# Attention's products with the values as float32r passes over a whole head

## The chip, the cores and the metric

The kernel runs on one core of a Trainium2 chip. The time is the device time of one execution in microseconds. The profile covers one execution; its span runs from the first to the last recorded instruction of the core.

## What is computed

Two layers, each `h += ½·SwiGLU(norm(h))`, `h += mixer(norm(h))`, `h += ½·SwiGLU(norm(h))`, then a last norm, for one sequence of 512 positions and width 1024, in float32. The change lies in layer 0's mixer, an attention with 8 heads of width 128 in which a small indexer picks 128 keys for each query:

```python
q, k, v, qi, ki, wi = jnp.split(h @ w_in, A_SPLITS, axis=-1)
...
_, idx = lax.top_k(score, top_k)
...
logits = (jnp.einsum('bthe,btkhe->bhtk', qb, kg) * scale + bias)
logits = jnp.where(valid[:, None], logits, -jnp.inf)
p = jax.nn.softmax(logits, axis=-1)
o = jnp.einsum('bhtk,btkhe->bthe', p, vg)
...
return out @ w_out
```

The kernel gathers nothing: it computes all causal logits and adds a mask of the chosen keys.

## The kernel before

Activations are held transposed: eight tiles H of 128 features by 512 positions. Most products are written as three TensorE passes in float32r: `mul3` (L345) multiplies the high part of the weights with the high and the low part of the activations, and the low part of the weights with the high part of the activations. A pair of parts comes from `split` (L369): ScalarE copies the number into a float32r tile (the high part), VectorE subtracts that from the number (the low part). Weights stream in 512 KB pieces on SyncE's queue; for each piece ScalarE writes the high part (L184) and another engine the low part (L187): VectorE as a rule, and GpSimd from L779 until the end of the heads (L945). A piece serves eight calls of `take`, and pieces are converted ahead of use, in the order of the program.

The schedule is written by hand: every engine runs its instructions in the order in which the program issues them, and waits on semaphores where data is not there yet.

In `mixer_a` (L694) the program first computes the indexer's scores and, for each block of 128 queries but the first, 16 rounds of `max8` and `match_replace` on VectorE, which leave the mask. These steps wait in a list, `W.background`, out of which each weight conversion takes some. Between them `v_half` (L817) computes the values for 512 of the 1024 columns at a time, and ScalarE copies them out of PSUM with the norm's scale (L829) into V, four float32 tiles of 128 positions by 1024.

Then come the heads. The list `blocks` (L920) has 32 entries, a head and a block b of 128 queries; block b sees (b+1)·128 keys. One round of the loop (L922) issues, in this order:

- `normalize` (L885) for the entry two rounds back: VectorE's reciprocal (L888) and a scaling of the probabilities (L889);
- `logits` (L869) for this round's entry: TensorE's product of queries and keys in float32 (L872), VectorE's scale and bias (L876), VectorE's mask and maximum (L879), VectorE's negation of the maximum (L881), ScalarE's exponential with its sum (L882);
- two steps of `filler` (L857): three-pass products for the queries and keys of later heads, later for the output projection `out_first`;
- `turn` (L891) for the entry three rounds back: b+1 transposes on TensorE (L896) into one bank, and ScalarE's copy into the tile pT (L898);
- one more filler step in odd rounds;
- `values` (L903) for the entry four rounds back: b+1 float32 products of the values with pT (L908) into 128 columns of the bank po. After a head's last block `split` writes its output from po into two float32r tiles, oh and ol (L911 to L913).

```python
mm(po[0][:, b * P:(b + 1) * P], V[j][:, h * P:(h + 1) * P], pT[:, j * P:(j + 1) * P],
   start=j == 0, stop=j == b)
```

PSUM has eight banks in two rings of four: "aux" serves logits and transposes, "acc" the fillers and po. The output projection reads oh and ol of all heads; after the loop its remaining products follow (L943 to L955).

Of the kernel before, what the change touches and what calls it, by code (L numbers as in the profile page):

```python
# [12 lines left out]
F32 = mybir.dt.float32  # L13
F32R = mybir.dt.float32r
I32 = mybir.dt.int32
AF = mybir.ActivationFunctionType
ALU = mybir.AluOpType
PSUM = bass.MemoryType.PSUM

P = 128  # L20
D = 1024
S = 512
KD = D // P
NT = S // P
# [217 lines left out]
def tile_trunk(ctx: ExitStack, tc, specs_out, xT, wst, gT, gl, rel, onehot, bu, bv, lng, lnb, wspT, bsp, out):  # L242
    nc = tc.nc
# [9 lines left out]
    def uname(s):  # L253
        counter[0] += 1
        return f"{s}_{counter[0]}"

    def pad(pool, size):

        pool.tile([P, size // 4], F32, name=uname("pad"))
# [3 lines left out]
    mm = nc.tensor.matmul  # L263
    def bank(tag="acc"):
        return psum.tile([P, 512], F32, tag=tag, bufs=4, name=uname(tag))
# [103 lines left out]
    def split(src, hi, lo):  # L369
        nc.scalar.activation(hi, src, AF.Copy)  # L370
        nc.vector.tensor_tensor(lo, src, hi.bitcast(F32), op=ALU.subtract)
# [322 lines left out]
    def mixer_a(dist, next_norm):  # L694
# [8 lines left out]

        with ExitStack() as stack:
            ap = stack.enter_context(tc.tile_pool(name="mixa", bufs=1))
            V = [ap.tile([P, D], F32, name=f"v{t}") for t in range(NT)]
            score = {b: ap.tile([P, (b + 1) * P], F32, name=f"score{b}") for b in range(1, NT)}
            pad(ap, 288)
            rq = ap.tile([P, NT], F32, name="rq")
            caus = ap.tile([P, P], F32, name="caus")  # L710
            nc.gpsimd.memset(caus, 0.0)
# [3 lines left out]
            R = {}  # L715
# [43 lines left out]
            with tc.tile_pool(name="mixai", bufs=1) as ip:  # L759
                ki = ip.tile([P, S], F32, name="ki")  # L760
                kh = ip.tile([P, S], F32R, name="kh")
                kl = ip.tile([P, S], F32R, name="kl")
                wiT = ip.tile([IDX_DIM + IDX_HEADS, S], F32, name="wiT")
                wi = ip.tile([P, NT, IDX_HEADS], F32, name="wi")
                lo, hi = slice(0, IDX_DIM), slice(IDX_DIM, P)
                wr = slice(IDX_DIM, IDX_DIM + IDX_HEADS)
                nc.vector.tensor_copy(wiT[wr], kw[wr])
                nc.vector.tensor_tensor(ki[lo], kw[lo], rb[lo], op=ALU.mult)
                nc.scalar.activation(ki[hi], ki[lo], AF.Copy)
                split(ki, kh, kl)  # L770
                pad(ip, 128)
                qs = []
                for h in range(IDX_HEADS):
                    a, b = (lo, hi) if h % 2 == 0 else (hi, lo)
                    t = ip.tile([P, S], F32R, name=f"qs{h}")
                    nc.scalar.activation(t[a], pq[h // 2][a], AF.Copy)
                    nc.vector.tensor_tensor(t[b], pq[h // 2][a], t[a].bitcast(F32), op=ALU.subtract)
                    qs.append(t)
                W.lo_engine = nc.gpsimd  # L779

                for i, _ in enumerate(projections(range(1), "acc")):
                    if i != KD:
                        continue
                    rc = R["c"]
                    nc.vector.tensor_scalar(rq, rc, P ** -0.5, None, op0=ALU.mult)
                    pw = bank("aux")
                    for t in range(NT):
                        nc.tensor.transpose(pw[:, t * IDX_HEADS:(t + 1) * IDX_HEADS], wiT[wr, t * P:(t + 1) * P],
                                            ident[wr, wr])
                    for t in range(NT):  # L790
                        nc.vector.tensor_scalar(wi[:, t], pw[:, t * IDX_HEADS:(t + 1) * IDX_HEADS], rc[:, t:t + 1],
                                                rc[:, t:t + 1], op0=ALU.mult, op1=ALU.mult)
                    w = wi.rearrange("p t h -> p (t h)")
                    nc.vector.tensor_scalar(w, w, IDX_HEADS ** -0.5, None, op0=ALU.mult)

                def score_one(b, h):
                    n = (b + 1) * P
                    sc = score[b]
                    ps = bank()
                    q = qs[h][:, b * P:(b + 1) * P]  # L800
                    mm(ps[:, :n], q, kh[:, :n], start=True, stop=False)
                    mm(ps[:, :n], q, kl[:, :n], start=False, stop=True)
                    rl = ip.tile([P, S], F32, tag="rl", bufs=3, name=uname("rl"))
                    nc.scalar.activation(rl[:, :n], ps[:, :n], AF.Relu, scale=IDX_DIM ** -0.5)
                    w = wi[:, b, h:h + 1]
                    if h == 0:
                        nc.vector.tensor_scalar(sc, rl[:, :n], w, None, op0=ALU.mult)
                    else:
                        nc.vector.scalar_tensor_tensor(sc, rl[:, :n], w, sc, op0=ALU.mult, op1=ALU.add)
                    if h == IDX_HEADS - 1:  # L810
                        nc.gpsimd.affine_select(out=sc[:, b * P:], in_=sc[:, b * P:], compare_op=ALU.is_ge,
                                                fill=NOT_CAUSAL, base=0, pattern=[[-1, P]], channel_multiplier=1)
                        W.background = interleave(W.background, top_k(b))

                todo = [(b, h) for b in range(1, NT) for h in range(IDX_HEADS)]

                def v_half(c, tag):  # L817
                    banks = [bank(tag) for _ in range(NT)]
                    for k in range(KD):
                        wh, wl = W.take(*[spec_a(k, 2 * D + c * 512 + i * P) for i in range(4)])  # L820
                        for t in range(NT):
                            xh, xl = XH[k][:, t * P:(t + 1) * P], XL[k][:, t * P:(t + 1) * P]
                            mm(banks[t], xh, wh, start=k == 0, stop=False)
                            mm(banks[t], xl, wh, start=False, stop=False)
                            mm(banks[t], xh, wl, start=False, stop=k == KD - 1)
                        for _ in range(min(3, len(todo))):
                            score_one(*todo.pop(0))
                    for t in range(NT):
                        nc.scalar.activation(V[t][:, c * 512:(c + 1) * 512], banks[t], AF.Copy,  # L829
                                             scale=R["c"][:, t:t + 1])  # L830

                W.pops = 2
                v_half(0, "aux")
                W.pops = 6
                v_half(1, "acc")
                assert not todo

            vp = stack.enter_context(tc.tile_pool(name="mixav", bufs=1))
            pad(vp, 352)
            O = {}  # L840
# [50 lines left out]
            def turn(h, b):  # L891
                n = (b + 1) * P
                pr, _ = prob.pop((h, b))
                ps = bank("aux")
                for j in range(b + 1):
                    nc.tensor.transpose(ps[:, j * P:(j + 1) * P], pr[:, j * P:(j + 1) * P], ident)  # L896
                pT = vp.tile([P, S], F32, tag="pT", bufs=2, name=uname("pT"))
                nc.scalar.activation(pT[:, :n], ps[:, :n], AF.Copy)  # L898
                turned[h, b] = pT

            po = [None]

            def values(h, b):  # L903
                if b == 0:
                    po[0] = first[3] if first else bank()
                pT = turned.pop((h, b))
                for j in range(b + 1):
                    mm(po[0][:, b * P:(b + 1) * P], V[j][:, h * P:(h + 1) * P], pT[:, j * P:(j + 1) * P],  # L908
                       start=j == 0, stop=j == b)
                if b == NT - 1:  # L910
                    oh = vp.tile([P, S], F32R, name=f"oh{h}")  # L911
                    ol = vp.tile([P, S], F32R, name=f"ol{h}")
                    split(po[0], oh, ol)  # L913
                    O[h] = (oh, ol)

            for h in range(3):
                load_bias(h)
# [4 lines left out]
            for i in range(len(blocks) + lag + 1):  # L922
                if 2 <= i < len(blocks) + 2:
                    normalize(*blocks[i - 2])
                if i < len(blocks):
                    logits(*blocks[i])
                    h, b = blocks[i]
                    if b == NT - 1 and h + 3 < HEADS:
                        load_bias(h + 3)
                filler(2)  # L930
                if lag <= i < len(blocks) + lag:
                    turn(*blocks[i - lag])
                filler(i % 2)
                if i > lag:
                    values(*blocks[i - lag - 1])
                if i == 4:
                    W.pops = 1

# [309 lines left out]
```

## Time and profile before

| | |
|---|---|
| median of 3 runs | 2093.56 us (2093.43 to 2094.03) |
| profiled execution | 2093.53 us, span 2091.7 us |
| TensorE matmul | 2076.6 us busy, 99% of the span |
| TensorE weight load | 1844.4 us, 88% |
| VectorE | 1476.7 us, 71% |
| ScalarE | 894.3 us, 43% |
| GpSimd | 78.1 us, 4% |
| DMA | 209.72 MB, 100 GB/s on average |

In the trace TensorE's instructions are PE (matmul) and PEld (weight load), VectorE is DVE, ScalarE is ACT, GpSimd is POOL. A float32 product stands as two PE instructions. A matmul's recorded length includes its way through the array, and matmuls overlap; what one costs in a row of others is the distance from start to start. VectorE and ScalarE instructions also overlap a little, so there, too, the distance between starts counts. The stretch with the heads runs from 488 to 592 us of the span.

### The profile page before, as it was taken

What the parts mean: (1) busy time and instruction counts of PE and PEld (TensorE: products, weight loads), DVE (VectorE), ACT (ScalarE), POOL (GpSimd) and SP (SyncE); (2) the same over time, 40 slices, a digit from 0 to 9 for tenths busy, and PEclk for the clock granted to TensorE, in tenths of its full rate; (3) what the DMA queues carried; (4) which work ended last, traced back from release to release, by engine and by line L of the source; (5) the groups of instructions that cost most, each with busy time, mean ns of one, the idle gap of its engine ahead of it and who ended that gap; (6) DMA issues with size and microseconds to landing.
All of it is one profiled execution on the core that took longest, in us unless ns stands there. A gap on an engine that the chain in (4) does not pass through costs nothing.

```text
span 2091.7 us, 29771 instructions
## 1 busy us (share of the span) xinstructions
PE 2076.6 (99%) x12252; PEld 1844.4 (88%) x12252; DVE 1476.7 (71%) x2046; ACT 894.3 (43%) x1157; POOL 78.1 (4%) x57
## 2 busy tenths in 40 slices
PE   8999999999999999999999999999999999999998
PEld 7989898888888999898989999888888888989897
DVE  7768686597767678677968677645846466778676
ACT  6535344434446345354625344432323245535253
POOL 0000000143200000000000000000000000000000
PEclk9999999999999999999999999999999999999999
DMA  4233332222123222222333222422222222323321
GB/s 174 98 117 109 112 110 92 100 96 90 68 72 110 101 101 101 101 101 82 111 106 107 101 102 81 152 91 91 91 101 83 89 91 91 111 94 109 110 93 71
DMA packets 59001, 209.72 MB, mean 100 GB/s; under 512 B 6824, under 2 KB 6872, under 8 KB 58736
## 3 DMA queue, kind: packets, MB, share of 16 engines
q1 hardware_dynamic: 55584, 198.73, 27.4%
q0 software_dynamic: 1408, 5.38, 0.8%
q10 hardware_dynamic: 1872, 3.70, 0.5%
q8 instruction: 96, 1.57, 0.3%
q14 instruction: 41, 0.34, 0.1%
HBM read 205.67 MB, written 4.74 MB: 101 GB/s over the span
## 4 chain that ended last, share of the span: by engine, by line
PE 97%; DVE 2%; ACT 1%; issue 0%; ACTq 0%; DVEq 0%
PE acc L348 16%; PE acc L349 16%; PE acc L350 16%; PE aux L348 12%; PE aux L350 12%; PE aux L349 12%; PE acc L990 1%; PE aux L992 1%; PE aux L990 1%; PE acc L992 1%; PE acc L991 1%; PE aux L991 1%; PE aux L1040 1%; PE acc L908 1%; PE aux L872 1%; PE aux L896 0%
## 5 line engine op out<-in xcount | busy, mean ns | idle before, releaser
L187 DVE TENSOR_TENSOR wlo<-raw,whi 128x1024 fp32r<-128x1024 f32 (+1 forms) x382 | 463.4, 1218 | 296.7 <-ACT whi L184 296.3
L184 ACT ACTIVATE whi<-raw 128x1024 fp32r<-128x1024 f32 (+1 forms) x409 | 426.2, 1050 | 470.4 <-PE acc L349 192.0
L348 PE MATMUL acc<-xh,whi 128*128 128x512 f32 (+1 forms) x864 | 299.2, 346 | 1.7 <-ACT xh L309 1.6
L349 PE MATMUL acc<-xl,whi 128*128 128x512 f32 (+1 forms) x864 | 289.5, 335 | 1.1 <-DVE xl L310 1.1
L350 PE MATMUL acc<-xh,wlo 128*128 128x512 f32 (+1 forms) x864 | 289.1, 335 | 0.0
L348 PE MATMUL aux<-xh,whi 128*128 128x256 f32 (+1 forms) x616 | 196.9, 320 | 0.0
L350 PE MATMUL aux<-xh,wlo 128*128 128x256 f32 (+1 forms) x616 | 196.5, 319 | 0.0
L349 PE MATMUL aux<-xl,whi 128*128 128x256 f32 (+1 forms) x616 | 196.4, 319 | 0.0
L348 PEld LDWEIGHTS acc<-xh,whi 128*128 128x128 f32 x864 | 164.8, 191 | 20.0 <-ACT xh L309 2.6
L349 PEld LDWEIGHTS acc<-xl,whi 128*128 128x128 f32 x864 | 165.0, 191 | 18.7 <-DVE xl L310 2.0
L350 PEld LDWEIGHTS acc<-xh,wlo 128*128 128x128 f32 x864 | 164.8, 191 | 16.9
L348 PE MATMUL acc<-th,whi 128*128 128x256 f32 x608 | 172.4, 284 | 0.0
L350 PE MATMUL acc<-th,wlo 128*128 128x256 f32 x608 | 172.1, 283 | 0.0
L349 PE MATMUL acc<-tl,whi 128*128 128x256 f32 x608 | 172.0, 283 | 0.0
L348 PE MATMUL aux<-th,whi 128*128 128x256 f32 x544 | 154.0, 283 | 0.0
L349 PE MATMUL aux<-tl,whi 128*128 128x256 f32 x544 | 154.0, 283 | 0.0
L350 PE MATMUL aux<-th,wlo 128*128 128x256 f32 x544 | 154.0, 283 | 0.0
L348 PE MATMUL acc<-yh,whi 128*128 128x512 f32 x328 | 127.7, 389 | 0.0
L349 PE MATMUL acc<-yl,whi 128*128 128x512 f32 x328 | 127.7, 389 | 0.0
L348 PE MATMUL aux<-yh,whi 128*128 128x512 f32 x328 | 127.6, 389 | 0.0
L349 PE MATMUL aux<-yl,whi 128*128 128x512 f32 x328 | 127.6, 389 | 0.0
L350 PE MATMUL acc<-yh,wlo 128*128 128x512 f32 x328 | 127.6, 389 | 0.0
(292 smaller groups left out, 4404.9 us busy)
## 6 DMA issues: line engine op xcount, KB each, us to landing
raw<-in_wst SPq DMA_DIRECT2D x372, 512.0 KB, 3.2
dist<-dist_rows ACTq DMA_DIRECT2D x8, 320.0 KB, 4.2
h<-in_xT SPq DMA_DIRECT2D x8, 256.0 KB, 6.4
tb<-dist POOLq DMA_DIRECT2D x8, 256.0 KB, 3.9
bias<-in_bv POOLq DMA_DIRECT2D x1, 1536.0 KB, 7.5
raw<-in_wst SPq DMA_DIRECT2D x2, 256.0 KB, 3.5
wT<-in_wspT POOLq DMA_DIRECT2D x1, 512.0 KB, 9.3
bs<-in_bsp POOLq DMA_DIRECT2D x1, 512.0 KB, 11.4
```

The source lines that it names most:

```text
L184: self.nc.scalar.activation(hi[:, s], src[:, s], AF.Copy)
L187: self.lo_engine.tensor_tensor(lo[:, s], src[:, s], hi[:, s].bitcast(F32), op=ALU.subtract)
L348: mm(ps, wh, xh, start=first, stop=False, **kw)
L349: mm(ps, wh, xl, start=False, stop=False, **kw)
L350: mm(ps, wl, xh, start=False, stop=last, **kw)
L872: mm(ps[:, :n], QK[h, 0][:, b * P:(b + 1) * P], QK[h, 1][:, :n], start=True, stop=True)
L908: mm(po[0][:, b * P:(b + 1) * P], V[j][:, h * P:(h + 1) * P], pT[:, j * P:(j + 1) * P], start=j == 0, stop=j == b)
L990: mm(banks[t], xh, wh, start=k == 0, stop=False)
L991: mm(banks[t], xl, wh, start=False, stop=False)
L992: mm(banks[t], xh, wl, start=False, stop=k == KD - 1)
L1040: mm(ps[:, t * P:(t + 1) * P], V[t][:, d * P:(d + 1) * P], wT[:, g, :], start=True, stop=True)
```

## The change

The values are kept in two float32r parts instead of one float32 tile: for each half of the columns a high and a low tile, with four heads, four blocks of positions and 128 columns each. ScalarE writes the high part from PSUM with the norm's scale, VectorE the low part from PSUM, the scale and the high part. The transposed probabilities of a head are also kept in two parts, in tiles with 13 places of 128 columns. Block b's transposes go to places b, b+3, ..., b+3b, so that the queries which see key block j lie next to each other from place 4j on. ScalarE copies the transposes into the high tile as before (now rounded), and VectorE writes the low tile from PSUM and the high tile. The products are done once a head, after its last block: for each key block j three passes over all queries from block j on, 512, 384, 256 and 128 columns wide, which accumulate in one bank. The head's output parts go where the head's values were.

```diff
-            V = [ap.tile([P, D], F32, name=f"v{t}") for t in range(NT)]
             score = {b: ap.tile([P, (b + 1) * P], F32, name=f"score{b}") for b in range(1, NT)}
-            pad(ap, 288)
+            pad(ap, 448)
+            V = [[ap.tile([P, 4, NT, P], F32R, name=f"v{part}{c}") for part in "hl"] for c in range(2)]
+            pad(ap, 352)
...
                     for t in range(NT):
-                        nc.scalar.activation(V[t][:, c * 512:(c + 1) * 512], banks[t], AF.Copy,
-                                             scale=R["c"][:, t:t + 1])
+                        ps, r = banks[t].rearrange("p (h d) -> p h d", d=P), R["c"][:, t:t + 1]
+                        hi, lo = (v[:, :, t] for v in V[c])
+                        nc.scalar.activation(hi, ps, AF.Copy, scale=r)
+                        nc.vector.scalar_tensor_tensor(lo, ps, r, hi.bitcast(F32), op0=ALU.mult, op1=ALU.subtract)
...
-                pT = vp.tile([P, S], F32, tag="pT", bufs=2, name=uname("pT"))
-                nc.scalar.activation(pT[:, :n], ps[:, :n], AF.Copy)
-                turned[h, b] = pT
-
-            po = [None]
-
-            def values(h, b):
                 if b == 0:
-                    po[0] = first[3] if first else bank()
-                pT = turned.pop((h, b))
-                for j in range(b + 1):
-                    mm(po[0][:, b * P:(b + 1) * P], V[j][:, h * P:(h + 1) * P], pT[:, j * P:(j + 1) * P],
-                       start=j == 0, stop=j == b)
-                if b == NT - 1:
-                    oh = vp.tile([P, S], F32R, name=f"oh{h}")
-                    ol = vp.tile([P, S], F32R, name=f"ol{h}")
-                    split(po[0], oh, ol)
-                    O[h] = (oh, ol)
+                    turned[h] = [vp.tile([P, 13, P], F32R, tag="pT" + part, bufs=2, name=uname("pT")) for part in "hl"]
+
+                hi, lo = (x[:, b:4 * b + 1:3] for x in turned[h])
+                ps = ps[:, :n].rearrange("p (j q) -> p j q", q=P)
+                nc.scalar.activation(hi, ps, AF.Copy)
+                nc.vector.tensor_tensor(lo, ps, hi.bitcast(F32), op=ALU.subtract)
+
+            def values(h):
+                po = first[3] if first else bank()
+                ph, pl = (x.rearrange("p a q -> p (a q)") for x in turned.pop(h))
+                vh, vl = (x[:, h % 4] for x in V[h // 4])
+                for j in range(NT):
+                    s, m = slice(j * P, S), slice(4 * j * P, (3 * j + NT) * P)
+                    o, end = po[:, s], j == NT - 1
+                    mm(o, vh[:, j], ph[:, m], start=j == 0, stop=False, skip_group_check=True)
+                    mm(o, vh[:, j], pl[:, m], start=False, stop=False, skip_group_check=True)
+                    mm(o, vl[:, j], ph[:, m], start=False, stop=end, skip_group_check=True)
+
+                oh, ol = (x.rearrange("p t q -> p (t q)") for x in (vh, vl))
+                split(po, oh, ol)
+                O[h] = (oh, ol)
...
-                if i > lag:
-                    values(*blocks[i - lag - 1])
+                if i > lag and blocks[i - lag - 1][1] == NT - 1:
+                    values(blocks[i - lag - 1][0])
```

## Rows read from the trace of the kernel before

**Rows 1.** The page's chain that ended last, by engine.

```profile
PE 97%; DVE 2%; ACT 1%; issue 0%; ACTq 0%; DVEq 0%
```

**Rows 2.** Stages: stretch, its us, busy of PE, PEld, DVE, ACT, POOL, clock, DMA.

```profile
497.21:510.25 13.04, 12.70 (x69) 10.17 (x68) 8.96 (x24) 6.05 (x15) 5.27 (x3) 1.00 0.18 62
...
572.93:585.27 12.34, 12.34 (x71) 10.06 (x69) 8.63 (x25) 5.66 (x17) 2.38 (x1) 1.00 0.13 45
585.27:592.40 7.13, 7.05 (x48) 6.07 (x46) 3.68 (x5) 3.02 (x5) 2.47 (x1) 1.00 0.22 76
```

**Rows 3.** The chain in order of time: start, us, link; one block's value products.

```profile
521.93 0.89 PE acc L908 x8
```

**Rows 4.** Timeline of PE (start us, us): the warm-up, and two passes of 256.

```profile
2.91 5.38 PE L289 MATMUL aux<-ones_r 128*128 128x128 f32 x24 [2.91 <-ACT ones_r L286]
...
700.03 0.28 PE L349 MATMUL aux<-tl,whi 128*128 128x256 f32 x1
700.15 0.28 PE L350 MATMUL aux<-th,wlo 128*128 128x256 f32 x1
```

**Rows 5.** Timeline of DVE in one head, and the end of another.

```profile
512.48 0.15 DVE L888 RECIPROCAL st<-st 128x1 f32<-128x1 f32 x1
...
513.72 0.15 DVE L881 TENSOR_SCALAR st<-st 128x1 f32<-128x1 f32 x1
...
515.36 0.15 DVE L881 TENSOR_SCALAR st<-st 128x1 f32<-128x1 f32 x1
...
515.62 0.29 DVE L889 TENSOR_SCALAR pr<-pr,st 128x128 f32<-128x128 f32 x1
516.43 0.62 DVE L876 SCALAR_TENSOR_TENSOR lg<-aux,rq,tb 128x384 f32<-128x384 f32 x1 [0.52 <-PE aux L872]
...
517.69 0.16 DVE L881 TENSOR_SCALAR st<-st 128x1 f32<-128x1 f32 x1
...
517.95 0.35 DVE L889 TENSOR_SCALAR pr<-pr,st 128x256 f32<-128x256 f32 x1
519.78 0.75 DVE L876 SCALAR_TENSOR_TENSOR lg<-aux,rq,tb 128x512 f32<-128x512 f32 x1 [1.49 <-PE aux L872]
...
521.30 0.15 DVE L881 TENSOR_SCALAR st<-st 128x1 f32<-128x1 f32 x1
...
572.08 0.15 DVE L881 TENSOR_SCALAR st<-st 128x1 f32<-128x1 f32 x1
573.76 0.69 DVE L371 TENSOR_TENSOR ol<-acc,oh 128x512 fp32r<-128x512 f32 x1 [1.53 <-ACT oh L370]
```

**Rows 6.** Timeline of ACT in the first of these heads.

```profile
513.91 0.40 ACT L882 ACTIVATE pr<-lg,st 128x128 f32<-128x128 f32 x1 [2.07 <-DVE st L881]
...
514.31 0.36 ACT L898 ACTIVATE pT<-aux 128x256 f32<-128x256 f32 x1
515.55 0.51 ACT L882 ACTIVATE pr<-lg,st 128x256 f32<-128x256 f32 x1 [0.88 <-DVE st L881]
...
516.06 0.47 ACT L898 ACTIVATE pT<-aux 128x384 f32<-128x384 f32 x1
...
516.91 1.05 ACT L184 ACTIVATE whi<-raw 128x1024 fp32r<-128x1024 f32 x1
517.88 0.61 ACT L882 ACTIVATE pr<-lg,st 128x384 f32<-128x384 f32 x1
...
518.49 0.58 ACT L898 ACTIVATE pT<-aux 128x512 f32<-128x512 f32 x1
```

**Rows 7.** Groups by line: busy us, mean ns of one, idle before; VectorE subtracting 256 columns.

```profile
L457 DVE TENSOR_TENSOR u<-m,u 128x256 f32<-128x256 f32 x16 | 6.7, 418 | 0.0
```

**Rows 8.** Timeline: GpSimd's subtraction and a scaling on DVE beside it.

```profile
568.13 2.37 POOL L187 TENSOR_TENSOR wlo<-raw,whi 128x1024 fp32r<-128x1024 f32 x1 [7.97 <-ACT whi L184]
...
568.50 2.15 DVE L889 TENSOR_SCALAR pr<-pr,st 128x256 f32<-128x256 f32 x1
```

**Rows 9.** Timeline of DVE ahead of the heads.

```profile
488.19 0.69 DVE L733 TENSOR_TENSOR qk<-aux,rb 128x512 f32<-128x512 f32 x1 [4.00 <-PE aux L350]
```

## The prediction

> **What bounds the kernel now.** I read first the chain that ended last: 97% of the span is TensorE [rows 1], so a step counts only where it makes TensorE work or wait. Then the stages. A head of attention is four rounds, one for each block of 128 queries. From the second head's first logits on, when all steps of a round are under way, to the end of the last round with logits lie seven times four rounds: 585.27 - 497.21 = 88.06 us, 12.58 us a head, and TensorE is busy in nearly all of it; the drain behind them takes 7.13 us [rows 2]. Third, the queues of VectorE and ScalarE in one head [rows 5, 6]: each runs in program order and both are idle part of the time, but they hand work to each other. The reader should see there that VectorE's last logits step of a round releases ScalarE's exponential, that ScalarE's copy of transposes lies behind that exponential, and that at the end of a head VectorE stands idle 1.53 us for ScalarE's rounded output, with the next round's reciprocal queued behind it.
>
> **TensorE's part.** Removed: 20 passes of 128 columns a head (10 products, two passes each in the trace). Eight of them take 0.89 us on the chain [rows 3], 0.111 each, so 2.22 us a head. Added: 12 float32r passes a head, three each of 512, 384, 256 and 128 columns. Passes of 256 columns follow each other at 0.12 us [rows 4]; by columns 512, 384 and 256 together take 0.54. For 128 columns the nearest row is the warm-up: 24 float32r passes in 5.2 us at the start, 0.216 each [rows 4], twice a removed pass; I read that as the lower of TensorE's two clocks, 1.2 GHz, and take half at 2.4, 0.108 (bounds: 0.06 by columns, 0.111 as the removed pass). Three times 0.65 is 1.94 us, a gain of 0.28 us a head, 2.2 us in all (3.4 with the low bound). That is all that TensorE can win.
>
> **The values' rounding.** Each half of V keeps four ScalarE copies and gains four VectorE operations of 512 columns that read PSUM; the nearest row is the first logits step of 512, 0.75 long [rows 5], about 0.67 from start to start: 8 x 0.67 = 5.4 us. They enter the top-k backlog on VectorE. Behind that backlog VectorE now waits 4.00 us for TensorE [rows 9]; the first 5.4 - 4.0 = 1.4 us late logits are mostly taken up by VectorE's waits in the next rounds. I take 0.3 us, bounds 0 and 1.4.
>
> **The new subtraction in every round.** The copy of the transposes on ScalarE stays; VectorE gains 32 subtractions that read the transposes and this copy. In a round for block b, VectorE's order is: reciprocal and scaling of block b+2 (of the round two before), three logits steps of b, subtraction of block b+1 (three before). So the subtraction waits for ScalarE's copy, which lies behind the exponential of this very round, which waits for the logits steps just issued. Behind the subtraction wait the next round's reciprocal, scaling and logits on VectorE, hence the next exponential on ScalarE, and the scaled blocks that TensorE has to transpose. What was overlapped becomes a serial loop. Its rounds, from rows of one undisturbed head:
>
> VectorE, reciprocal to the small step that releases the exponential [rows 5]: round 0, 513.72 - 512.48 = 1.24; round 1, 515.36 - 513.79 = 1.57 (the reciprocal, left out of the rows, starts 0.07 behind the step before, as in all rounds); round 2, 0.19 for the reciprocal, 0.21 for the scaling (0.29 long, next start 0.08 earlier), 517.69 - 516.43 = 1.26, together 1.66; round 3, 0.19 + 0.27 + (521.30 - 519.78) = 1.98.
> Then 0.19 to the exponential's start (513.72 to 513.91), the exponential's time until the copy starts (0.40, 0.51, 0.61 for 128, 256, 384), the copy (0.36, 0.47, 0.58 for 256, 384, 512) [rows 6] and 0.03. A subtraction of 512 from PSUM is the output's own, 0.69 [rows 5], of 256 about 0.42 [rows 7]; 0.08 less from start to start: 0.61, 0.48 (between), 0.34.
> Round 0: 1.24 + 0.19 + 0.40 + 0.36 + 0.03 + 0.34 = 2.56. Round 1: 1.57 + 0.19 + 0.51 + 0.47 + 0.03 + 0.48 = 3.25. Round 2: 1.66 + 0.19 + 0.61 + 0.58 + 0.03 + 0.61 = 3.68. Round 3 also has the head's output: from that small step to the output's subtraction 573.76 - 572.08 = 1.68 where ScalarE waits for nobody [rows 5], within which the subtraction of 128 fits; 1.98 + 1.68 + 0.61 = 4.27. Sum 13.8 us a head, where TensorE needs 12.58 - 0.28 = 12.3. Seven heads: 96.4 us.
>
> What else lies on this loop. ScalarE converts weights, 1.05 long, 0.95 to the next start [rows 6]: eight in the seven heads, of which by the trace five stand between an exponential and the copy behind it: 4.8 us (bounds 0 and 7.6). One query copy stands there too, 0.5 (a copy of 512 less the overlap). GpSimd's half of each conversion blocks VectorE's steps that use SBUF alone: a scaling of 256 takes 2.15 us instead of 0.35 [rows 5] while GpSimd subtracts [rows 8]. By the trace seven of nine such subtractions cost VectorE time, 0.6 to 1.8 us each, 9.4 in all, and I keep that (bounds 0, as the new waits may absorb it, and nine times 1.8, 16.2). The keys' multiplications go into the wait for ScalarE: nothing, or 0.6 each if they fall behind it. No DMA is added, and the bias loads on GpSimd's queue have three buffers. The output's new place and the removed output tiles add no instruction; the pads have none.
>
> Sum. VectorE enters the seven heads with TensorE, at about 497.0. The first new wait, in the round before, adds 2.7 us (the 1.68 without the output's copy of 0.6, and 0.5, 0.95 and 0.2 for a query copy, a conversion and a subtraction of 128); with the 0.3 it enters at 500.0. Plus 96.4 + 4.8 + 0.5 + 9.4 = 111.1: 611.1. Drain: two scalings, each followed by transposes, copy and subtraction, then 1.94 us of values: 0.5 + 0.4 + 0.6 + 0.4 + 0.6 + 0.6 + 2.0, 5.1 us, to 616.2, where TensorE now goes on at 592.4 [rows 2]. So +23.8 us on the profiled execution's 2093.53 us (span 2091.7; the median of the runs shown is 2093.56): 2117.3. TensorE's own gain is inside this: it only waits longer.
>
> TensorE's clock. The granted clock is 1.00 through these heads, with TensorE all but never idle [rows 2]; with the loop it would be idle some 3.5 us in 16, in pieces of a round. The Trainium skill (TensorE: Matmul & The Clock Gate, section on the second failure mode, depth-cycling of the PSUM queue) says that a kernel whose TensorE idles briefly and often between groups of matmuls swings between the two clocks. No run here shows it. By the rows the sum is 2117.3; by that rule it is the clock rival below.
>
> **The rivals.** *Hidden.* VectorE and ScalarE would keep ahead of TensorE, the subtraction finding its copy ready, and only the passes count: 2093.5 - 2.2 = 2091.3 us, 2090.1 with the low bound. For it: VectorE has idle time in each head, and values are multiplied a round later than their transposes. Against: the order of the two queues; VectorE already waits 1.53 us behind an exponential once a head. It decides where the loop, with its conversions, falls under 12.3 us; the bare sum is 13.8, so a seventh of every wait priced above would have to be an overestimate and all the extras be absorbed.
> *The clock falls.* At 1.2 GHz TensorE's 12.3 us a head are 24.6, more than the loop's 15.9, so TensorE is busy throughout and should recover: if half of the seven heads ran so, 3.5 x (24.6 - 15.9) = 30 us more, 2148. For it: gaps in every head, which nowhere exist now. Against: the gaps are about a microsecond each.
>
> **How the numbers follow.** Loop 0.81, hidden 0.13, clock 0.06. The loop's own bounds: without conversions and GpSimd, 499.7 + 96.4 + 5.1 = 601.2, 8.8 us late, 2102.3; with conversions 7.6, GpSimd 16.2, a query copy 0.5, keys 2.4 and entry at 501.1, 501.1 + 123.1 + 5.1 = 629.3, 36.9 us late, 2130.4. A little beyond these, for the rounds that I composed from single rows: 2100 to 2133 holds the loop's 0.81. Changes within 0.2% (4.2 us), about what a measurement of this kernel can tell from none, hold the hidden case but for its low bound and absorbed noise: same 0.11, faster 0.03, slower 0.86.
>
> **What the profile would show.** Right: 32 subtractions on VectorE, most behind waits of about 1 us on ScalarE's copies; TensorE idle some 20 us or more between 497 and 617, released at the values by a subtraction and at transposes by scalings; heads 15 to 16 us apart; twelve float32r passes in about 1.9 us a head. Wrong: heads still 12 us apart with TensorE busy (hidden); a granted clock of 0.5 in the heads (clock); or transposes' copies on ScalarE that start ahead of the exponential of their round, which would break the loop.

## The result, and the profile after

The changed kernel takes 2127.59 us (median of 4 runs, 2126.91 to 2127.76), the kernel before, run beside it on the same chip, 2093.79 us. The ratio is 1.016, with a 95% interval of 1.0148 to 1.0173. The profiled execution took 2127.76 us, its span is 2126.0 us, 34.3 longer than before.

The page's busy times, and its chain by engine, which answers to [rows 1]:

```profile
PE 2087.1 (98%) x12188; PEld 1846.4 (87%) x12188; DVE 1497.6 (70%) x2086; ACT 893.9 (42%) x1157; POOL 77.9 (4%) x57
...
PE 89%; DVE 8%; ACT 2%; issue 1%; ACTq 0%; DVEq 0%
```

TensorE held 97% of the chain and holds 89% now. VectorE's 21 us of added work do not say where 34 us went: its busy share fell from 71% to 70%. The stages do, with the columns of [rows 2]: the whole stretch up to the last value pass, then three of the seven heads, then the drain.

```profile
497.25:626.89 129.64, 106.30 (x461) 79.57 (x460) 82.02 (x220) 45.30 (x113) 26.49 (x15) 0.92 0.17 55
498.06:515.83 17.77, 14.38 (x61) 10.54 (x60) 11.27 (x30) 6.29 (x15) 5.27 (x3) 0.90 0.20 65
...
549.01:565.83 16.82, 13.02 (x62) 9.45 (x62) 10.36 (x31) 5.83 (x15) 2.91 (x3) 1.00 0.15 47
565.83:584.39 18.56, 14.53 (x63) 10.87 (x62) 11.47 (x33) 6.92 (x17) 4.92 (x3) 0.87 0.18 60
...
617.86:626.89 9.03, 8.11 (x37) 6.32 (x38) 3.82 (x9) 3.20 (x7) 2.48 (x1) 0.85 0.15 58
```

The last value pass ends at 626.89, where it ended at 592.40 [rows 2]: all of the loss but 0.85 us, which came earlier and outside the change, lies in this stretch. From the first logits of a head to those of the next there are now 15.1 to 18.6 us, (617.86 - 498.06) / 7 = 17.1 on average, where there were 12.58. All four engines have idle time in every head: none is the bound by its work. What they wait for is in the groups of waits from 480 to 640 us (engine, line, what it waited for: us in total, times, longest):

```profile
ACT pr L885 <- DVE st L884: 87.2, 31, 6.1
DVE pT L906 <- ACT pT L905: 41.2, 32, 2.7
PEld acc L915 <- ACT pT L905: 17.5, 8, 4.1
...
PE acc L915 <- ACT pT L905: 14.2, 8, 3.7
...
PE aux L899 <- DVE pr L892: 7.8, 7, 2.3
...
DVE vl L371 <- ACT vh L370: 4.1, 8, 2.6
```

L906 is the new subtraction, L905 ScalarE's copy, L885 the exponential, L884 the small step that releases it. VectorE waits 41.2 us in 32 subtractions, one each round, and ScalarE 87.2 us for VectorE in 31: the two engines wait for each other by turns, which is what a serial loop looks like in such a list. Before the change, from 484 to 606 us, ScalarE waited less for this step, and VectorE waited for ScalarE's steps of the heads only at the heads' ends:

```profile
ACT pr L882 <- DVE st L881: 52.1, 28, 4.1
DVE ol L371 <- ACT oh L370: 16.0, 8, 3.4
```

That wait at a head's end (1.53 in [rows 5]) is now 0.2 to 0.4 in all heads but the last, since it is swallowed by the wait in front of it. One round on VectorE in the changed kernel shows the order that makes the loop:

```profile
521.85 0.15 DVE L891 RECIPROCAL st<-st 128x1 f32<-128x1 f32 x1
522.04 0.48 DVE L892 TENSOR_SCALAR pr<-pr,st 128x512 f32<-128x512 f32 x1
522.45 0.47 DVE L879 SCALAR_TENSOR_TENSOR lg<-aux,rq,tb 128x256 f32<-128x256 f32 x1
...
523.42 0.15 DVE L884 TENSOR_SCALAR st<-st 128x1 f32<-128x1 f32 x1
524.68 0.56 DVE L906 TENSOR_TENSOR pT<-aux,pT 128x384 fp32r<-128x384 f32 x1 [1.10 <-ACT pT L905]
525.15 0.15 DVE L891 RECIPROCAL st<-st 128x1 f32<-128x1 f32 x1
```

In these 3.3 us VectorE works 2.2. It issues the step that lets ScalarE start the exponential, and then stands 1.10 us until ScalarE has done that exponential and the copy queued behind it.

### The profile page after: what moved, and what is told of

It reads as the page before. It is cut to its first block, busy times and chain, and to the rows that moved or that the text cites. A ratio compares the mean times of both kernels' runs of the same rounds, so it can differ in the third digit from the quotient of the medians.

```text
span 2126.0 us, 29700 instructions
## 1 busy us (share of the span) xinstructions
PE 2087.1 (98%) x12188; PEld 1846.4 (87%) x12188; DVE 1497.6 (70%) x2086; ACT 893.9 (42%) x1157; POOL 77.9 (4%) x57
## 4 chain that ended last, share of the span: by engine, by line
PE 89%; DVE 8%; ACT 2%; issue 1%; ACTq 0%; DVEq 0%
PE acc L348 15%; PE acc L349 15%; PE acc L350 15%; PE aux L348 11%; PE aux L350 11%; PE aux L349 11%; DVE score L744 1%; PE acc L997 1%; PE aux L999 1%; PE acc L999 1%; PE acc L998 1%; PE aux L998 1%; PE aux L997 1%; PE aux L1047 1%; DVE m L741 1%
```

## The experiments

The theory: the wait of the subtraction for ScalarE's copy, which lies behind the exponential of the same round, makes a loop of VectorE and ScalarE that takes longer than TensorE's work. The rivals: VectorE's added work costs by its length; the new passes on TensorE cost; the values' rounding costs; TensorE's clock does it. The kernel before took 2093.95 to 2094.05 us beside these runs.

**The subtractions alone, in the kernel before.**

```diff
                 nc.scalar.activation(pT[:, :n], ps[:, :n], AF.Copy)
+                lo = vp.tile([P, S], F32R, tag="plo", bufs=1, name=uname("plo"))
+                nc.vector.tensor_tensor(lo[:, :n], ps[:, :n], pT[:, :n], op=ALU.subtract)
```

> The kernel before with only the 32 subtractions added, at the place where the changed kernel has them; their result is written to a tile that nothing reads. Values and products as before, float32. Theory (the subtraction's wait is the whole cost): 2120 to 2132 us. Rival (TensorE waits because it needs the low part in the products): no more than 2100 us, since nothing needs this result but the bank's release.

Measured 2123.98 us (2123.72 to 2124.26), ratio 1.0142 (1.0127 to 1.0158). The waits of this kernel, where L900 is the subtraction and L898 the copy:

```profile
ACT pr L882 <- DVE st L881: 84.1, 32, 4.1
DVE plo L900 <- ACT pT L898: 39.1, 31, 2.7
```

Nothing else of the change is in this kernel, and it has 30 of the 34 us, with the same pair of waits. At most the other 4 us can be due to the new passes, the rounding and the layouts.

**The change without the subtractions.**

```diff
-                nc.vector.tensor_tensor(lo, ps, hi.bitcast(F32), op=ALU.subtract)
...
-                    mm(o, vh[:, j], pl[:, m], start=False, stop=False, skip_group_check=True)
+                    mm(o, vh[:, j], ph[:, m], start=False, stop=False, skip_group_check=True)
```

> The changed kernel without the 32 subtractions and without their tiles; the second of the three passes multiplies with the high part again, so TensorE's passes are as in the changed kernel, and the low part of the probabilities is left out of the computation. Theory: no serial loop, TensorE bound, and what is left is its own gain and the values' rounding: 2089.5 to 2093 us. If the whole-row passes themselves, at the end of a head, make TensorE wait or slow its clock: 2100 us or more.

Measured 2092.32 us (2091.69 to 2092.56), ratio 0.9991 (0.9982 to 1.0). So all that the change does for TensorE is worth some 1.7 us, with the values' rounding in it; 2.2 were put down.

**A copy in the subtraction's place.**

```diff
-                nc.vector.tensor_tensor(lo, ps, hi.bitcast(F32), op=ALU.subtract)
+                nc.vector.tensor_copy(lo, ps)
```

> The changed kernel in which the 32 subtractions are replaced, at the same place of VectorE's queue, by a copy of the transposes from PSUM that does not read ScalarE's copy: the low part is then not the low part but the whole number, so the subtraction is left out of the computation. VectorE's work stays about the same, the wait for ScalarE goes. Theory (the wait): 2090 to 2102 us. Rival (the work): 2120 to 2128 us.

Measured 2127.07 us (2126.98 to 2127.69). This run missed its aim. The copy doesn't use ScalarE's result, yet it waits for it as the subtraction did:

```profile
DVE pT L906 <- ACT pT L905: 39.4, 30, 2.7
```

Both engines read the same PSUM bank, the one thing that the two steps share in the program, and the wait is what it would be if the two reads were kept in the program's order. The Trainium skill (PSUM — Partial Sum Buffer, section on bank collisions) says that accesses of two engines to one bank must not fall together, reads included. The wait here agrees with an order kept for that; that the bank is the cause is argued and not shown, since no run has the two reads in different banks, or the same bank without the order.

**The same copy ahead of ScalarE's.**

```diff
+                nc.vector.tensor_copy(lo, ps)
                 nc.scalar.activation(hi, ps, AF.Copy)
-                nc.vector.tensor_tensor(lo, ps, hi.bitcast(F32), op=ALU.subtract)
```

> The changed kernel with the subtraction replaced by a VectorE copy of the transposes out of PSUM into the low tile, issued ahead of ScalarE's copy, so that it waits for the transposes only (the low part of the probabilities is left out of what is computed; VectorE's time for it is about that of the subtraction, and its place in VectorE's queue is the same). Theory (it is the wait for ScalarE's copy, which lies behind the exponential, and not VectorE's additional work that costs): VectorE's waits for ScalarE in the rounds vanish, 2093 to 2106 us, heads 12.3 to 14.3 us apart, with what is left of the wait at a head's end. Rival (VectorE's 32 additional operations cost by their length): 2120 or more, with waits that have gone elsewhere.

Measured 2097.49 us (2096.33 to 2098.57), ratio 1.0017 (1.0008 to 1.0026). The same work of VectorE, at the same place between the logits steps and the next reciprocal: 30 us go with the order of two instructions. This separates the wait from the work most clearly. What the work costs by itself is about the 5.2 us between this kernel and the one without any such step, 2092.32. What is left of VectorE's waits for ScalarE is the one at a head's end, about as much as before the change; and in four rounds ScalarE's copy (now L906) waits for VectorE's (now L905), the order turned round:

```profile
DVE vl L371 <- ACT vh L370: 15.5, 8, 3.5
...
ACT pT L906 <- DVE pT L905: 3.8, 4, 2.3
```

**The subtraction one round later**, behind the next round's logits steps; nothing is left out.

```diff
...
-                nc.vector.tensor_tensor(lo, ps, hi.bitcast(F32), op=ALU.subtract)
+                late.append(lambda: nc.vector.tensor_tensor(lo, ps, hi.bitcast(F32), op=ALU.subtract))
...
                         load_bias(h + 3)
+                while late:
+                    late.pop(0)()
```

> The changed kernel with one thing moved: each of the 32 subtractions that write the low part of the transposed probabilities is issued one round later, behind the next round's logits steps, where ScalarE's copy has long been written. Same instructions, same operands. Theory (the wait in VectorE's queue makes a serial loop of VectorE and ScalarE): nearly all of the loss goes, 2090 to 2102 us, heads 12 to 13 us apart, TensorE idle under 8 us in the heads. Rival (VectorE has simply too much work in the heads): 2115 us or more. Rival (TensorE's passes over whole rows, or its clock by itself, cost the time): 2120 us or more.

Measured 2104.89 us (2104.84 to 2104.99), ratio 1.0051 (1.0036 to 1.0066), above what the theory gave. The loop is open, but two other waits have grown, in the list of the changed kernel 4.1 us (VectorE, L371) and 1.4 (TensorE, L916):

```profile
DVE vl L371 <- ACT vh L370: 20.8, 8, 3.0
...
PEld acc L916 <- DVE pT L906: 11.2, 8, 3.1
PE acc L916 <- DVE pT L906: 8.2, 7, 2.8
...
DVE pT L906 <- ACT pT L905: 2.3, 3, 1.2
```

Which of the two is the rest of the loss? The first is longer, and I took it. The next run moves it.

**The output's low part one round later as well.**

```diff
-                split(po, oh, ol)
-                O[h] = (oh, ol)
+                nc.scalar.activation(oh, po, AF.Copy)
+
+                def low():
+                    nc.vector.tensor_tensor(ol, po, oh.bitcast(F32), op=ALU.subtract)
+                    O[h] = (oh, ol)
+                late.append(low)
...
```

> The changed kernel with both kinds of VectorE steps that wait for ScalarE issued one round later, behind the next round's logits steps: the subtractions of the transposes, and the low part of a head's output. Nothing is left out. With the subtractions alone so moved it took 2104.9 us, heads 14.28 us apart. Theory (the rest of that loss is the wait at a head's end, 20.8 us in eight): 2090.5 to 2096 us, heads 12.3 to 12.8 us apart, VectorE's waits for ScalarE under 5 us in all. Rival (the loss moves to TensorE, which now waits in the values for the subtraction of the last block, or VectorE's work is too much in itself): 2100 to 2105, heads still 14 us apart.

Measured 2102.82 us (2102.52 to 2104.21), ratio 1.0044 (1.0032 to 1.0057). The theory of the head's end fell: its wait went from 20.8 to 4.2 us, and brought 2 us. The run without the subtractions had shown as much: there the same wait is 20.5 us in all, and that kernel lost nothing. TensorE's wait for the last block's subtraction, at the second value pass (L916), stayed:

```profile
PEld acc L916 <- DVE pT L906: 10.2, 8, 3.1
...
PE acc L916 <- DVE pT L906: 7.2, 6, 2.8
```

A wait of an engine that is not the bound costs nothing, however long it is; the 7.2 us on TensorE are on the path.

**The value products one round later as well**, so that this subtraction is done before TensorE comes to it.

```diff
...
-                if i > lag and blocks[i - lag - 1][1] == NT - 1:
-                    values(blocks[i - lag - 1][0])
+                if i > lag + 1 and blocks[i - lag - 2][1] == NT - 1:
+                    values(blocks[i - lag - 2][0])
```

> The kernel with both steps issued one round later, and the products with the values also one round later, so that TensorE does not come to them before the subtraction of the head's last block. Nothing is left out. Theory (with every wait of a round taken out, TensorE's passes alone count): 2090 to 2093.5 us, at or 2 us under the kernel before; TensorE all but never idle in the heads. Rival (the products had found their parts ready already, or a later output delays the output projection): no better than with both steps moved alone, or up to 3 us slower.

Measured 2096.28 us (2094.6 to 2096.6), ratio 1.0009 (1.0 to 1.0017), above the 2093.5 that the theory gave at most. TensorE's 7.2 us at L916 are 2.0, and from the fourth head's first logits to the last's it is never idle; a head takes 12.09 us, less than before the change [rows 2]:

```profile
508.40:524.16 15.76, 13.93 (x61) 11.09 (x60) 12.75 (x31) 6.61 (x17) 5.77 (x4) 0.89 0.16 53
524.16:536.25 12.09, 12.09 (x61) 9.69 (x60) 10.52 (x31) 5.46 (x14) 2.87 (x2) 1.00 0.30 96
...
586.13:596.00 9.87, 8.05 (x45) 6.32 (x44) 3.47 (x8) 3.50 (x9) 2.36 (x1) 1.00 0.16 54
```

The gain of those heads is given back in the first row, where VectorE comes late, TensorE waits 1.82 us and its granted clock is 0.89, and in the last, where nothing is left that could cover a head's last steps.

**Other work in the drain.** The output projection's fourth column for heads 0 to 6, which came behind the loop, is issued ahead of the last head's values.

```diff
                 if i > lag + 1 and blocks[i - lag - 2][1] == NT - 1:
+                    if blocks[i - lag - 2][0] == HEADS - 1:
+                        for _ in fill:
+                            pass
+                        W.lo_engine = nc.vector
+                        extra = bank("aux")
+                        for k in range(HEADS - 1):
+                            mul3(extra, W.take(spec_o(k, 3)), O[k], k == 0, False)
                     values(blocks[i - lag - 2][0])
...
```

> The kernel with subtractions, output and value products one round later, and in addition the output projection's fourth column for heads 0 to 6 (21 passes of 512 columns, 4.8 us) issued ahead of the last head's values instead of behind them. Nothing is left out. In the kernel without this TensorE idles 2.7 us behind the last logits (0.91 and 0.91 for the sixth and seventh head's parts and copies, the rest between the last transposes) while this work stands behind the values. Theory (what is left of the loss is in the first two heads and in this drain): 2093 to 2094.8 us, 1.5 to 3 us less than without it, about the kernel before. Rival (the drain is set by weights or by VectorE): no change, 2096.

Measured 2095.53 us (2094.42 to 2096.72), ratio 1.0009 (1.0 to 1.0018). This is inconclusive, and above the 2094.8 that the theory gave at most: the medians differ by 0.75 us and the runs of each kernel by 2. The trace shows that one wait was exchanged for another: the 0.91 us at the last values is gone, and the same 0.91 us stands at the last head's output, which the projection now needs at once.

**The same without the low parts of the values.** The line for them in `v_half` is taken out and the third pass reads the high part.

> The same without the eight VectorE operations for the low parts of the values; the third pass uses the high part again, so the low part of the values is left out of what is computed, at unchanged work of TensorE. Theory (in the first heads VectorE comes late from the rounding of the values and catches up one head later, where TensorE waited 1.8 us at a lower clock): 2090.5 to 2092.5 us, two to three us less than with them, heads 12.1 us apart from the first. Rival (the delay in the first heads is that of GpSimd's subtractions and of the heads' own work): 2093 to 2095, no less.

Measured 2093.75 us (2093.29 to 2094.3), ratio 0.9999 (0.999 to 1.0008): 1.8 us less than with them, under the two to three expected, and above the 2092.5 that the theory gave at most. TensorE's wait in the first values is 1.17 instead of 1.83 us, so the rounding is a part of the lateness in the first heads, and not the only one.

**The changed kernel without the low parts of the values.** The same line taken out of the kernel as changed.

> The changed kernel without the eight VectorE operations that write the low parts of the values (L833); the third pass of each product uses the high part again, so the low part of the values is left out of what is computed, while TensorE's work stays the same. Theory (the loop of VectorE and ScalarE in the heads sets the end, the values' rounding costs next to nothing): 2126 to 2127.6 us, at most 1.5 under the changed kernel; VectorE's wait ahead of the heads comes back, heads stay 16 to 17 us apart. Rival (the 5.4 us of rounding delay the heads one for one): about 2122. Hidden rival: 2127.6, nothing at all.

Measured 2125.89 us (2125.74 to 2126.16), 1.7 us under the changed kernel: a little more than the 1.5 at most that I gave it, far from the 5.4 of a full delay.

**The low parts of the weights on VectorE** in the heads, in the kernel as changed: GpSimd's subtractions go, nine in the loop and eleven in all, and VectorE gets them.

```diff
+            W.lo_engine = nc.vector
             blocks = [(h, b) for h in range(HEADS) for b in range(NT)]
```

> The changed kernel, in which from the first round of the heads on VectorE instead of GpSimd writes the low parts of the weights (nine pieces in the heads, about 1.2 us of VectorE each). Theory (GpSimd's subtractions lengthen VectorE's steps on the loop by about 1.3 us a piece, and five of the new VectorE subtractions fall beside ScalarE's copy of the transposes, for which VectorE waits anyway, so that they cost about 0.65 each and the others 1.15): minus 12, plus 3.3, plus 4.6, about 4 us less than the changed kernel, 2122 to 2125.5 us. Rival (GpSimd's blocking is absorbed by the waits and costs little): the new VectorE work comes on top, 2130 to 2137.

Measured 2124.54 us (2124.09 to 2124.81), 3.05 less than the changed kernel. VectorE has eleven subtractions of 1.2 us more, and the kernel is faster. VectorE's busy time in the whole program is even 1496.0 us, 1.6 less than in the changed kernel, since its other steps are no longer lengthened. So GpSimd's subtractions did lie on the loop, and part of VectorE's own fall into the wait for ScalarE, as its waits show, 24.9 us where they were 41.2:

```profile
DVE pT L906 <- ACT pT L905: 24.9, 23, 1.3
```

No version that computes everything came out faster than the kernel before.

## Why the prediction came out as it did

The forecast was the loop, 2117.3 us; it came to 2127.59, inside the range and 10 us above the forecast. The mechanism was right: 32 subtractions that wait, the exponential behind VectorE, TensorE idle, heads further apart. One sign differed: at the values TensorE is released by ScalarE's copy (14.2 us in 8 waits at L915, whose first pass needs the high part only) and hardly by the subtraction (1.4 us at L916). The subtractions alone reproduce it, and the order of two instructions takes it away.

**The rounds.** The round sums held. One head on VectorE between reciprocals that follow a subtraction:

```profile
519.23 0.15 DVE L891 RECIPROCAL st<-st 128x1 f32<-128x1 f32 x1
...
521.85 0.15 DVE L891 RECIPROCAL st<-st 128x1 f32<-128x1 f32 x1
...
525.15 0.15 DVE L891 RECIPROCAL st<-st 128x1 f32<-128x1 f32 x1
...
526.19 2.74 DVE L882 CUSTOM_DVE_ANT_0 lg<-lg,score 128x384 f32<-128x384 f32 x1
...
531.05 0.15 DVE L891 RECIPROCAL st<-st 128x1 f32<-128x1 f32 x1
...
535.38 0.15 DVE L891 RECIPROCAL st<-st 128x1 f32<-128x1 f32 x1
```

They are 2.62, 3.30, 5.90 and 4.33 us. In the third, VectorE's mask step took 2.74 us beside a GpSimd subtraction, 2.18 more than its usual 0.56; without that it is 3.72. The forecast had 2.56, 3.25, 3.68 and 4.27: about 0.05 short in each round of this head; over 28 rounds that is an estimated 1.5 us.

**What was mis-sized.** The last value pass was forecast to end at 616.2 and ended at 626.89. The 10.7 us go by the steps:

- *Entry*: VectorE enters the heads at 501.80, not 500.0. Of these 1.8 us, 0.85 is that the second head's first logits on TensorE came at 498.06 instead of 497.21; 0.8 of it is there at 50 us of the program already, outside the change (0.1 to 1.05 in the other runs). The rest is the values' rounding: VectorE's first logits step was at 491.65 instead of 488.80, 2.0 late besides that start, where 1.4 was expected and 0.3 priced. In the kernel as changed without the low parts of the values VectorE enters at 500.41, and the whole gains 1.7 us: above the upper bound of 1.4.
- *The loop*, 501.80 to VectorE's drain round at 619.34, is 117.5 us, not 111.1. The nine steps of VectorE that GpSimd lengthened took 12.1 us more than their usual time, not 9.4: in the stretched schedule all nine hit a step, not seven. Six conversions stood between exponential and copy, not five (0.9), two query copies and not one (0.5), and one key multiplication came behind a subtraction (0.6). With the estimate for the rounds that is 6.2 of the 6.4.
- *The drain*, 7.55 us, not 5.1. Its first six passes of 512 columns took 620.52 - 617.86 = 2.66 us at a granted clock of 0.58, mostly the lower of the two levels, 1.2 GHz, where 0.23 each at the higher, 2.4 GHz, make 1.4. The last head's transposes are queued behind them. That is up to 1.3 of the 2.45. The rest is TensorE's queue: from 617.86 to 626.89 it is idle for 0.92 us only, all of it at the last values. Nine more passes of the output projection, from 620.65 to 622.13 and from 622.37 to 623.15, stand between the last head's transposes, and the forecast's drain, a sum of VectorE's and ScalarE's steps with the transposes, had no term for them. How much each of these terms is worth alone was not tested.

```profile
617.86:621.00 3.14, 3.14 (x11) 2.42 (x12) 1.48 (x4) 1.79 (x5) 1.28 (x1) 0.58 0.00 0
621.00:626.89 5.89, 4.97 (x28) 3.89 (x27) 2.35 (x5) 1.41 (x3) 1.20 (x1) 1.00 0.24 89
```

```profile
620.52 0.38 PE L899 MATMUL aux<-ident,pr 128*128 128x128 f32 x2
...
622.13 0.49 PE L899 MATMUL aux<-ident,pr 128*128 128x128 f32 x3
...
623.15 0.60 PE L899 MATMUL aux<-ident,pr 128*128 128x128 f32 x4
624.44 0.49 PE L915 MATMUL acc<-pT,vh 128*128 128x512 f32 x1 [0.69 <-ACT pT L905]
```

**TensorE's part.** Twelve passes a head in about 1.9 us were forecast. In the head whose values start at 546.56, at a granted clock of 1.00, they follow each other 0.23 apart at 512 columns, 0.175 at 384, 0.12 at 256:

```profile
547.62 0.39 PE L917 MATMUL acc<-pT,vl 128*128 128x512 f32 x1
547.85 0.34 PE L915 MATMUL acc<-pT,vh 128*128 128x384 f32 x1
548.03 0.34 PE L916 MATMUL acc<-pT,vh 128*128 128x384 f32 x1
...
548.49 0.28 PE L916 MATMUL acc<-pT,vh 128*128 128x256 f32 x1
548.61 0.28 PE L917 MATMUL acc<-pT,vl 128*128 128x256 f32 x1
548.73 0.22 PE L915 MATMUL acc<-pT,vh 128*128 128x128 f32 x1
548.79 0.28 PE L916 MATMUL acc<-pT,vh 128*128 128x128 f32 x1
548.90 0.27 PE L917 MATMUL acc<-pT,vl 128*128 128x128 f32 x1
549.01 0.43 PE L875 MATMUL aux<-qk,qk 128*128 128x128 f32 x2
```

Of the 128-column passes the first costs 0.06 and the others 0.11, the two bounds that were given. At these distances twelve take 1.85 us.

**The hidden rival** needed VectorE to find the copy ready. It never did: 32 waits in 32 subtractions. That it could have been so with another order is what the runs with later subtractions show. (The "seventh" in the forecast's case against it is a ninth of the loop's sum, 1.5 of 13.8 us; no chance there is worked out from it.)

**The clock rival** came in part: the granted clock is 0.92 over the stretch, 0.87 to 1.00 by head and 0.85 in the drain. The Trainium skill's rule of briefly idle matmul groups (TensorE: Matmul & The Clock Gate, section on depth-cycling) is borne out as far as the clock goes, where the prediction had no row for it. It is not the cause of the loss. With the subtractions alone the clock stayed at 1.00 in seven of eight windows of 15 to 18 us, up to 605 us, and the loss was 30 us; and the loop's terms add up without it, since TensorE waited at their ends. Only in the drain, where VectorE waits for transposes, does a row show a cost, the up to 1.3 us told above.

## What to carry to other kernels

A step that waits for another engine belongs in its queue behind the work that this engine is waiting for, not right behind what it depends on in the text of the program: here one subtraction a round, issued a round too early, was worth 23 of 34 us, and its length about 5. Before a change is costed by busy time, write the two queues side by side for one round and look for a cycle; its length is the sum of rows that the old trace already has. And when a wait is taken away, look first for the wait on the bounding engine, not for the longest one.

## What was not expected

Two engines' reads of one PSUM bank came in the order in which the program has them: a copy that needed nothing of ScalarE's result waited 39.4 us for it, and issued first it left the time 3.5 us above the kernel before.

TensorE's clock did not follow from the pause alone. In the kernel with values a round later TensorE paused 1.82 us ahead of the pass at 512.44, and the clock of that head was 0.89; in the kernel with the drain filled it paused 1.83 us at the same pass, and stayed at 1.00:

```profile
508.52:522.73 14.21, 12.38 (x61) 9.68 (x60) 12.78 (x31) 6.51 (x17) 5.76 (x4) 1.00 0.19 59
```

The same 61 passes kept TensorE busy for 13.93 us in the one and 12.38 in the other. What decided between them the runs don't show, and it need not be the kernel. Of the 22 runs of the two kernels, the ten of 2096.28 us and more have a granted clock of 0.997 or 0.998 over the whole run, the eight from 2095.0 to 2095.7 have 0.999; but the four shortest, 2094.4 to 2094.7, have 0.998 too. So the clock goes with part of the spread of 2 us and does not explain all of it.
